# Transposing x and B for the state-space scan: on TensorE against the identity, or on DVE in blocks of 32 with a pass through DRAM

## The chip, the cores and the metric

The kernel runs on one core of a Trainium2 chip. The metric is the device time of one launch in microseconds (us). A core has five engines that work side by side, each through its own list of instructions in a fixed order: TensorE (PE in the profile, with its weight loads listed as PEld), VectorE (DVE), ScalarE (ACT), GpSimd (POOL) and SyncE (SP), which here only issues DMAs. An instruction waits for semaphores that other engines or DMAs raise; while it waits, everything behind it on the same engine waits too. DMAs move data between DRAM and the on-chip SBUF over 16 shared DMA engines ("rings" below). PSUM is the small memory that PE writes its products to.

## What is computed

One layer of a hybrid decoder, on 512 tokens (S) of 1024 channels (D), in float32: a Mamba-2 mixer and a sliding-window attention side by side, then a SwiGLU. The change touches the Mamba-2 part, the chunked scan. Cut to that:

```python
def ssd_chunked_scan(xh, dt, a, b_ssm, c_ssm):
    X = (xh * dt[..., None])                      # [chunk, T=128 tokens, group, head, 64]
    dA = dt * a
    a_cum = jnp.cumsum(dA, axis=-1)
    Lmat = jnp.exp(segsum(dA))
    CB = jnp.einsum('bclgn,bcsgn->bcgls', Cc, Bc)
    y_diag = jnp.einsum('bcgels,bcsgep->bclgep', Lmat * CB[:, :, :, None], X)
    decay_states = jnp.exp(a_cum[..., -1:] - a_cum)
    states = jnp.einsum('bclgn,bcgel,bclgep->bcgepn', Bc, decay_states, X)
    # h: running sum of states over the chunks, decayed by exp(a_cum[..., -1])
    y_off = jnp.einsum('bclgn,bcgepn,bcgel->bclgep', Cc, h_in, jnp.exp(a_cum))
    return y_diag + y_off
```

There are 4 groups of 8 heads and 4 chunks of 128 tokens, so 16 pairs of group and chunk. Each such pair is called a chunk here and numbered i = 0 to 15 (group i // 4, chunk c = i % 4 of the group).

## The kernel before

**The large products.** Every large matrix product is split into float32r halves, and one 128x512 step is three matmuls: high by high, high by low, low by high (`mm3`, L147 to L151). Weights come in units of 128x1024. The class `Units` (L110 to L145) loads a unit by SP into `w_raw` (four buffers), casts it on ACT to `w_hi` (L135) and takes the rest on DVE, `w_lo` (L136); three units are split ahead of the one in use, and four more can lie raw. One `product` (L275) is one unit: 8 steps of 3 matmuls, 24 in all, into one of three PSUM buffers of the pool psA, and then an eviction. PE's other results go to five PSUM buffers of the pool psX.

**Who sets the order.** The order on PE is the order of the code, since PE is under a manual schedule (L78). The order on DVE, ACT, POOL and SP is chosen by the scheduler from dependencies and buffers. Large products that nothing in the scan needs soon are put into a queue, the `Filler` (L153 to L183), as generators. A call `fill(us)` steps the one in front, at 0.65 us a step (one step is three matmuls); `all_done(name)` steps until all of that name are through. So the small matmuls of the scan stand on PE between blocks of filler matmuls, which cover their latency.

**The convolutions.** x, B and C of a group come from six units (`g_xbc`, L355 to L377). Their PSUM result is evicted through a causal convolution of four taps: ACT makes the first (L368, `cacc`), DVE adds three (L371), and ACT applies SiLU. This leaves channels on the partitions and tokens along the row: `bc_f` for B and C, four tiles `xs_f` for x. The six units of the next group are filler in the rounds of the present one.

**The scan.** Its main loop (L941 to L973) runs one round per chunk i. Its parts:

- `ssd_pre(i)` (L737): SP loads `L`, 512 KB, one row of DRAM broadcast to all partitions (L743), and from c = 1 on `E` in two DMAs (L750). POOL masks `L` (L754), and ACT takes 8 exps of it (L759).
- `ssd_a(i)` (L761): PE makes `ps_cb` from B and C (L774), ACT copies it to `cb`, and DVE multiplies `L` by it (L778). PE transposes the four 128x128 blocks of x by matmuls with the identity, `ps_x` (L781). DVE multiplies by dt, which gives X in two instructions (L784). For c < 3, whose state goes on, PE also transposes B (`ps_bt`, L790), ACT copies that to `bt` (L792), and POOL multiplies X by the decay, `Xd` (L795).
- `ssd_b(i)`, first half (L800): for c < 3 the state, `ps_st` = `bt` times `Xd` (L809), to which the state before is added in `h_st`; for c > 0 the part from the earlier chunks, `ps_yo` (L825). Second half: `ps_yd`, from X and L (L834), added to the output `y_g` by DVE.

Ahead of the loop stand `ssd_pre` of chunks 0 and 1, `ssd_a(0)` and a `fill(4.0)`, at which the filler's queue is still empty, so it issues nothing. A round i then calls `ssd_pre(i+2)`, `ssd_a(i+1)`, `fill`, the first half of `ssd_b(i)`, `fill`, the second half, and `fill`: 6 us each (5 in the last group). At c = 3, `all_done` makes sure that the next group's convolutions are through before `ssd_a` of its first chunk. What goes on just before the scan is the product `yb` of the attention's output, evicted into `tB` on DVE (L414).

Of the kernel before, what the change touches and what calls it, by code (L numbers as in the profile page):

```python
# [11 lines left out]
F32 = mybir.dt.float32  # L12
# [50 lines left out]
def kernel(  # L63
# [13 lines left out]
    nc = tc.nc  # L77
# [32 lines left out]
    class Units:  # L110
# [29 lines left out]
        def next(self, unit, kt=KD, ahead=None):  # L140

            assert self.order[self.pos] == unit, (self.pos, self.order[self.pos], unit)
            self.prepare(self.pos + (self.ahead if ahead is None else ahead))
            self.pos += 1
            return tuple(a.rearrange("p (k n) -> p k n", k=kt) for a in self.split.pop(self.pos - 1))  # L145
# [7 lines left out]
    class Filler:  # L153
# [19 lines left out]
        def fill(self, us):  # L173
            self.owed += us / 0.65
            while self.owed >= 1.0 and self.step():
                self.owed -= 1.0
            self.owed = min(self.owed, 1.0)
# [56 lines left out]
    h_d = dram.tile([S, D], F32, name="h_d")  # L234
    a_d = dram.tile([P, P], F32, name="a_d")
    e_d = dram.tile([P, P], F32, name="e_d")


    def xbc(g):
# [29 lines left out]
    def axt(shape, name):  # L269
        return psX.tile(shape, F32, name=name, tag="ax")  # L270
# [82 lines left out]
    xbc_t = {}  # L353
# [378 lines left out]
    er = e_d.rearrange("(g j c t) l -> g c j (t l)", g=NG, j=2, c=NT)  # L732
    dt5, dec5, cd5, nac5 = cols(dtv), cols(dec), cols(cdec), cols(nac)

    z_t, y_t, yn_t, L_t, E_t, a_t, h_t = {}, {}, {}, {}, {}, {}, {}

    def ssd_pre(i):  # L737

# [18 lines left out]
        for j in range(2):  # L757
            for t in range(4):
                nc.scalar.activation(L[:, j, t], L[:, j, t], AF.Exp, bias=nac5[:, g, j, c, t:t + 1], scale=1.0)  # L759

    def ssd_a(i):  # L761

        g, c = divmod(i, NT)
        cs = slice(c * P, (c + 1) * P)
        b_f, c_f = xbc_t[g, 0], xbc_t[g, 1]
        xs = [xbc_t[g, 2 + t] for t in range(4)]
        if c == 0:
            y = sd.tile([P, 4, S], F32, name="y_g", tag="y_g", bufs=1)
            y_t[g] = y
            for t in range(4):  # L770
                nc.scalar.mul(out=y[:, t], in_=xs[t], mul=pc[:, C_DS + 4 * g + t:C_DS + 4 * g + t + 1])
        L = L_t[i]
        ps = axt([P, P], "ps_cb")
        nc.tensor.matmul(ps, b_f[:, cs], c_f[:, cs], start=True, stop=True)  # L774
        cb = sd.tile([P, P], F32, name="cb", tag="cb", bufs=2)
        nc.scalar.copy(out=cb, in_=ps)  # L776
        Lf = L.rearrange("p j t l -> p (j t) l")
        nc.vector.tensor_tensor(out=Lf, in0=Lf, in1=cb.unsqueeze(1).broadcast_to([P, 8, P]), op=ALU.mult)  # L778
        ps = axt([P, 4, 2, 64], "ps_x")
        for t in range(4):  # L780
            nc.tensor.transpose(ps[:, t].rearrange("p j d -> p (j d)"), xs[t][:, cs], ident)  # L781
        X = sd.tile([P, 4, 2, 64], F32, name="X", tag="X", bufs=2)
        for j in range(2):
            nc.vector.tensor_tensor(  # L784
                out=X[:, :, j], in0=ps[:, :, j],
                in1=dt5[:, g, j, c].unsqueeze(2).broadcast_to([P, 4, 64]), op=ALU.mult)
        bt = Xd = None
        if c < NT - 1:
            ps = axt([P, P], "ps_bt")
            nc.tensor.transpose(ps, b_f[:, cs], ident)  # L790
            bt = sd.tile([P, P], F32, name="bt", tag="bt", bufs=2)
            nc.scalar.copy(out=bt, in_=ps)  # L792
            Xd = sd.tile([P, 4, 2, 64], F32, name="Xd", tag="Xd", bufs=2)
            for j in range(2):
                nc.gpsimd.tensor_tensor(  # L795
                    out=Xd[:, :, j], in0=X[:, :, j],
                    in1=dec5[:, g, j, c].unsqueeze(2).broadcast_to([P, 4, 64]), op=ALU.mult)
        a_t[i] = (X, bt, Xd)

    def ssd_b(i):  # L800

        g, c = divmod(i, NT)
        cs = slice(c * P, (c + 1) * P)
        y, c_f, L = y_t[g], xbc_t[g, 1], L_t.pop(i)
        X, bt, Xd = a_t.pop(i)
        h_prev = h_t.pop(g, None)
        if c < NT - 1:
            pss = axt([P, 4, 2, 64], "ps_st")
            nc.tensor.matmul(  # L809
                pss.rearrange("p t j d -> p (t j d)"), bt, Xd.rearrange("p t j d -> p (t j d)"),  # L810
                start=True, stop=True)
            h = sd.tile([P, 4, 2, 64], F32, name="h_st", tag="h_st", bufs=2)
            h_t[g] = h
            if c == 0:
                nc.scalar.copy(out=h, in_=pss)
            else:
                for j in range(2):
                    nc.gpsimd.tensor_tensor(
                        out=h[:, :, j], in0=h_prev[:, :, j],
                        in1=cd5[:, g, j, c].unsqueeze(2).broadcast_to([P, 4, 64]), op=ALU.mult)  # L820
                nc.vector.tensor_add(h, h, pss)
        if c > 0:
            pso = axt([P, 4, P], "ps_yo")
            for t in range(4):
                nc.tensor.matmul(  # L825
                    pso[:, t], h_prev[:, t].rearrange("p j d -> p (j d)"), c_f[:, cs], start=True, stop=True)
            yo = sd.tile([P, 4, P], F32, name="yo", tag="tmp", bufs=3)
            nc.vector.tensor_mul(yo, pso, E_t.pop(i))
            nc.gpsimd.tensor_add(y[:, :, cs], y[:, :, cs], yo)
        yield  # L830
        psd = axt([P, 4, P], "ps_yd")
        for t in range(4):
            for j in range(2):
                nc.tensor.matmul(  # L834
                    psd[64 * j:64 * j + 64, t], X[:, t, j], L[:, j, t], start=True, stop=True)
        nc.vector.tensor_add(y[:, :, cs], y[:, :, cs], psd)
        yield
# [97 lines left out]
    def all_done(prefix):  # L935
        while any(str(n).startswith(prefix) for n, _ in filler.q):
            filler.step()

    ssd_pre(0)
    ssd_pre(1)  # L940
    ssd_a(0)  # L941
    fill(4.0)
    norm = iter(())
    for i in range(NG * NT):
        g, c = divmod(i, NT)
        if c == 0 and g > 0:
            norm = gate_norm(g - 1)
            next(norm)
        if c == 0:
            add_stage(g)  # L950
        f0, f1, f2 = F_SSD[g]
        if i + 2 < NG * NT:
            ssd_pre(i + 2)
        if i + 1 < NG * NT:
            if c == NT - 1:
                all_done(f"x{g + 1}")
            ssd_a(i + 1)
        fill(f0)
        b = ssd_b(i)
        next(b)  # L960

        slots = (0, 1, 1) if g == NG - 1 else (2, 3, 4)
        fill(f1)
        for _ in range(slots.count(2 * c)):
            next(norm, None)
        next(b)
        fill(f2)
        for _ in range(slots.count(2 * c + 1)):
            next(norm, None)
        if c == NT - 1:  # L970
# [196 lines left out]
    for f in range(2, NF):  # L1167
        pss = []
# [101 lines left out]
```

## Time and profile before

| | us |
|---|---|
| median of 3 runs | 1028.93 |
| lowest and highest | 1028.39, 1028.96 |
| the profiled execution, in the same terms | 1028.11 |
| its span in the trace | 1026.2 |

The mean clock granted to PE in the profiled execution is 0.999 of full speed. The first transpose `ps_x` of the scan starts at 237.0 us of the span, the last at 527.2.

How to read the rows that follow. A timeline row has the start (us from the span's start), the duration, the engine or queue, the line of the kernel, the instruction with its output and inputs, the shape, and how many instructions it groups; in square brackets is the idle time ahead of it and who ended it. SPq is SP's DMA queue: its rows are issues, not transfers. A stretch row has the stretch, its length, each engine's busy time with its instructions, the granted clock, the DMA engines' busy share and GB/s. A row of groups has the engine's busy time and the mean length of one instruction. Matmuls overlap on PE, so the distance of their starts, not their duration, is what one of them takes of PE's time. A wait row names who waited, for whom, how long in all, how many times, and the longest.

### The profile page before, as it was taken

To read this page: it belongs to the slowest core of one execution; us is meant where nothing else is said; L and a number is where in the kernel's file an instruction comes from. 1 tells how busy PE (TensorE), PEld (TensorE's weight loads), DVE (VectorE), ACT (ScalarE), POOL (GpSimd) and SP (SyncE) were. 2 spreads that over 40 slices of the span, in tenths; PEclk is the share of its full clock that TensorE was granted. 3 is DMA by queue.
4 is the path that set the end of the run, shared out by engine and by line. 5 is a ranking of instruction groups with operands and counts; after the bars stand their busy time and mean duration, and the time that the engine had idled before them with its cause. 6 is when DMAs were issued, how large, how long until landed. Compare 5 with 4: busy or idle time off the path is not lost.

```text
span 1026.2 us, 13200 instructions
## 1 busy us (share of the span) xinstructions
PE 1014.5 (99%) x5044; PEld 837.6 (82%) x5044; DVE 600.5 (59%) x835; ACT 505.8 (49%) x864; POOL 205.5 (20%) x195
## 2 busy tenths in 40 slices
PE   9999999999999999999999999999999999999997
PEld 7888888887887878888888888898888888888886
DVE  6789874534656764676664595646433333332765
ACT  6464566717666885783733542434332333322450
POOL 2011223723115113111223820390000000000000
PEclk9999999999999999999999999999999999999999
DMA  8211223544443334334322344316433333331471
GB/s 317 83 64 61 88 83 104 203 142 130 136 135 106 113 116 126 106 115 138 89 93 82 123 150 179 102 42 225 144 123 123 106 120 106 120 123 62 154 255 43
DMA packets 38799, 126.56 MB, mean 123 GB/s; under 512 B 4528, under 2 KB 5040, under 8 KB 38480
## 3 DMA queue, kind: packets, MB, share of 16 engines
q1 hardware_dynamic: 36080, 116.14, 34.7%
q0 software_dynamic: 2080, 7.47, 2.0%
q10 hardware_dynamic: 576, 2.10, 0.6%
q8 instruction: 40, 0.66, 0.2%
q14 instruction: 23, 0.19, 0.1%
HBM read 119.27 MB, written 6.42 MB: 122 GB/s over the span
## 4 chain that ended last, share of the span: by engine, by line
PE 86%; DVE 4%; ACT 3%; DMA 3%; issue 2%; POOL 1%; SPq 0%; DVEq 0%; POOLq 0%; ACTq 0%
PE ps_mm L149 13%; PE ps_mm L150 12%; PE ps_mm L151 12%; PE ps_ff L151 8%; PE ps_ff L149 8%; PE ps_ff L150 8%; PE ps_da L151 2%; PE ps_da L149 2%; PE ps_da L150 2%; DMA L<-a_d 2%; PE ps_db L151 2%; PE ps_db L150 2%; PE ps_db L149 2%; PE ps_mix L149 1%; PE ps_mix L151 1%
## 5 line engine op out<-in xcount | busy, mean ns | idle before, releaser
L135 ACT CAST w_hi<-w_raw 128x1024 fp32r<-128x1024 f32 x185 | 193.4, 1051 | 305.5 <-PE ps_ff L150 123.2
L136 DVE TENSOR_TENSOR w_lo<-w_raw,w_hi 128x1024 fp32r<-128x1024 f32 x185 | 240.5, 1305 | 154.1 <-ACT w_hi L135 151.9
L149 PE MATMUL ps_mm<-hT_hi,w_hi 128*128 128x512 f32 x504 | 203.3, 403 | 1.0 <-DVE cacc L371 1.0
L150 PE MATMUL ps_mm<-hT_lo,w_hi 128*128 128x512 f32 x504 | 196.8, 391 | 0.0
L151 PE MATMUL ps_mm<-hT_hi,w_lo 128*128 128x512 f32 x504 | 196.6, 390 | 0.0
L149 PE MATMUL ps_ff<-h2T_hi,w_hi 128*128 128x512 f32 (+1 forms) x384 | 143.2, 373 | 0.0
L150 PE MATMUL ps_ff<-h2T_lo,w_hi 128*128 128x512 f32 (+1 forms) x384 | 142.6, 371 | 0.0
L151 PE MATMUL ps_ff<-h2T_hi,w_lo 128*128 128x512 f32 (+1 forms) x384 | 142.6, 371 | 0.0
L149 PEld LDWEIGHTS ps_mm<-hT_hi,w_hi 128*128 128x128 f32 x504 | 94.7, 188 | 23.1 <-issue 5.6
L151 PEld LDWEIGHTS ps_mm<-hT_hi,w_lo 128*128 128x128 f32 x504 | 94.6, 188 | 20.3
L150 PEld LDWEIGHTS ps_mm<-hT_lo,w_hi 128*128 128x128 f32 x504 | 94.8, 188 | 18.2 <-issue 1.0
L150 PEld LDWEIGHTS ps_ff<-h2T_lo,w_hi 128*128 128x128 f32 x384 | 72.3, 188 | 12.6
L151 PEld LDWEIGHTS ps_ff<-h2T_hi,w_lo 128*128 128x128 f32 x384 | 72.3, 188 | 12.5
L149 PEld LDWEIGHTS ps_ff<-h2T_hi,w_hi 128*128 128x128 f32 x384 | 72.3, 188 | 12.4
L1117 DVE TENSOR_TENSOR sgf<-sgf,ps_ff 128x512 f32<-128x512 f32 x22 | 15.1, 685 | 68.4 <-PE ps_ff L151 68.4
L149 PE MATMUL ps_mm<-yh,w_hi 128*128 128x512 f32 x124 | 49.2, 397 | 0.0
L150 PE MATMUL ps_mm<-yl,w_hi 128*128 128x512 f32 x124 | 48.3, 390 | 0.0
L151 PE MATMUL ps_mm<-yh,w_lo 128*128 128x512 f32 x124 | 48.3, 389 | 0.0
L371 DVE SCALAR_TENSOR_TENSOR cacc<-ps_mm,pc,cacc 128x511 f32<-128x511 f32 (+2 forms) x54 | 39.9, 741 | 9.8 <-ACT cacc L368 9.2
L759 ACT ACTIVATE L<-L,nac 128x128 f32<-128x128 f32 x128 | 40.9, 391 | 6.2 <-POOL L L754 5.9
L778 DVE TENSOR_TENSOR L<-L,cb 128x1024 f32<-128x1024 f32 x16 | 21.5, 1343 | 38.4 <-ACT cb L776 21.6
L754 POOL TENSOR_SCALAR_AFFINE_SELECT L<-L 128x1024 f32<-128x1024 f32 x16 | 20.1, 1256 | 93.9 <-DMA L<-a_d 93.9
(267 smaller groups left out, 1700.2 us busy)
## 6 DMA issues: line engine op xcount, KB each, us to landing
w_raw<-in_wall_dram SPq DMA_DIRECT2D x187, 512.0 KB, 3.5
L<-a_d SPq DMA_DIRECT2D x16, 512.0 KB, 5.4
E<-e_d SPq DMA_DIRECT2D x24, 128.0 KB, 3.5
x_d<-x_sb POOLq DMA_DIRECT2D x4, 512.0 KB, 7.8
row<-x_d POOLq DMA_DIRECT2D x4, 512.0 KB, 5.1
h_d<-row POOLq DMA_DIRECT2D x4, 512.0 KB, 3.0
h_r<-h_d ACTq DMA_DIRECT2D x4, 512.0 KB, 5.4
out_dram<-y_o SPq DMA_DIRECT2D x7, 256.0 KB, 4.1
```

Of the source, the lines that this page charges most:

```text
L135: (copy or nc.scalar.copy)(out=hi, in_=w)
L136: self.last = (eng or nc.vector).tensor_sub(out=lo, in0=w, in1=hi.bitcast(F32))
L149: nc.tensor.matmul(ps, lh, rh, start=start, stop=False)
L150: nc.tensor.matmul(ps, lh, rl, start=False, stop=False)
L151: nc.tensor.matmul(ps, ll, rh, start=False, stop=stop)
L371: nc.vector.scalar_tensor_tensor(out=acc[:, d:], in0=ps[:, :S - d], scalar=pc[:, cw + 3 - d:cw + 4 - d], in1=acc[:, d:], op0=ALU.mult, op1 ...
L754: nc.gpsimd.affine_select(out=Lf, in_=Lf, pattern=[[0, 8], [1, P]], compare_op=ALU.is_ge, fill=-BIG, base=0, channel_multiplier=-1)
L759: nc.scalar.activation(L[:, j, t], L[:, j, t], AF.Exp, bias=nac5[:, g, j, c, t:t + 1], scale=1.0)
L778: nc.vector.tensor_tensor(out=Lf, in0=Lf, in1=cb.unsqueeze(1).broadcast_to([P, 8, P]), op=ALU.mult)
L1117: nc.vector.tensor_mul(sg, sg, pu)
```

## The change

PE makes neither `ps_x` nor `ps_bt` any more. A new function `ssd_x(i)` has DVE transpose x in blocks of 32x32: its `transpose` swaps rows and columns inside each block but leaves the blocks where they are. The result `T` (256 KB) is written by one DMA to a DRAM scratch `t_d`, and four DMAs read it back into `R`, 32 partitions each, so that the blocks land where the transposed matrix has them, in runs of 512 bytes. For c < 3 it does the same to B, through `Tb`, `b_d` (64 KB) and four reads into `bt` in runs of 128 bytes. All these DMAs are issued by SP. A second function `ssd_dt(i)` makes X out of `R` on DVE and `Xd` on POOL, as before apart from the source.

The calls: `ssd_x(0)` stands ahead of `ssd_a(0)`, `ssd_dt(0)` and `ssd_x(1)` behind the empty `fill(4.0)`. In round i, behind the first half of `ssd_b(i)`, stand `ssd_dt(i+1)` and `ssd_x(i+2)`. `ssd_x` of a group's first chunk needs the group's convolutions, so the `all_done` for them is called in the round of c = 2, not c = 3. `T` uses three buffers that other temporaries of the scan use too (tag "tmp"), `R` has one, `bt` two as before, and `Xd` one in place of two. Line numbers in the rows of the changed kernel are those of the changed file.

```diff
@@ -234,6 +234,8 @@
     h_d = dram.tile([S, D], F32, name="h_d")
     a_d = dram.tile([P, P], F32, name="a_d")
     e_d = dram.tile([P, P], F32, name="e_d")
+    t_d = dram.tile([NG * NT, P, 4, P], F32, name="t_d")
+    b_d = dram.tile([NG * NT, P, 4, 32], F32, name="b_d")
 
 
     def xbc(g):
@@ -732,7 +734,7 @@
     er = e_d.rearrange("(g j c t) l -> g c j (t l)", g=NG, j=2, c=NT)
     dt5, dec5, cd5, nac5 = cols(dtv), cols(dec), cols(cdec), cols(nac)
 
-    z_t, y_t, yn_t, L_t, E_t, a_t, h_t = {}, {}, {}, {}, {}, {}, {}
+    z_t, y_t, yn_t, L_t, E_t, R_t, X_t, Xd_t, bt_t, h_t = ({} for _ in range(10))
 
     def ssd_pre(i):
 
@@ -758,6 +760,52 @@
             for t in range(4):
                 nc.scalar.activation(L[:, j, t], L[:, j, t], AF.Exp, bias=nac5[:, g, j, c, t:t + 1], scale=1.0)
 
+    def ssd_x(i):
+
+        g, c = divmod(i, NT)
+        cs = slice(c * P, (c + 1) * P)
+
+        T = sd.tile([P, 4, 4, 32], F32, name="T", tag="tmp", bufs=3)
+        for t in range(4):
+            nc.vector.transpose(T[:, :, t], xbc_t[g, 2 + t][:, cs])
+
+        R = sd.tile([P, 4, 4, 32], F32, name="R", tag="R", bufs=1)
+        R_t[i] = R
+        nc.sync.dma_start(out=t_d[i], in_=T.rearrange("p b t s -> p b (t s)"))
+        for b in range(4):
+            nc.sync.dma_start(
+                out=R[32 * b:32 * b + 32].rearrange("r a t s -> r a (t s)"),
+                in_=t_d[i, :, b].rearrange("(a r) x -> r a x", r=32))
+        if c < NT - 1:
+            Tb = sd.tile([P, P], F32, name="Tb", tag="Tb", bufs=1)
+            nc.vector.transpose(Tb, xbc_t[g, 0][:, cs])
+            bt = sd.tile([P, P], F32, name="bt", tag="bt", bufs=2)
+            bt_t[i] = bt
+            nc.sync.dma_start(out=b_d[i], in_=Tb.rearrange("p (b s) -> p b s", b=4))
+            for b in range(4):
+                nc.sync.dma_start(
+                    out=bt[32 * b:32 * b + 32].rearrange("r (a s) -> r a s", a=4),
+                    in_=b_d[i, :, b].rearrange("(a r) s -> r a s", r=32))
+
+    def ssd_dt(i):
+
+        g, c = divmod(i, NT)
+        R = R_t.pop(i)
+        X = sd.tile([P, 4, 2, 64], F32, name="X", tag="X", bufs=2)
+        X_t[i] = X
+        for j in range(2):
+            nc.vector.tensor_tensor(
+                out=X[:, :, j].rearrange("p t (h s) -> p t h s", h=2),
+                in0=R[:, 2 * j:2 * j + 2].rearrange("p h t s -> p t h s"),
+                in1=dt5[:, g, j, c].unsqueeze(2).unsqueeze(3).broadcast_to([P, 4, 2, 32]), op=ALU.mult)
+        if c < NT - 1:
+            Xd = sd.tile([P, 4, 2, 64], F32, name="Xd", tag="Xd", bufs=1)
+            Xd_t[i] = Xd
+            for j in range(2):
+                nc.gpsimd.tensor_tensor(
+                    out=Xd[:, :, j], in0=X[:, :, j],
+                    in1=dec5[:, g, j, c].unsqueeze(2).broadcast_to([P, 4, 64]), op=ALU.mult)
+
     def ssd_a(i):
 
         g, c = divmod(i, NT)
@@ -776,38 +824,17 @@
         nc.scalar.copy(out=cb, in_=ps)
         Lf = L.rearrange("p j t l -> p (j t) l")
         nc.vector.tensor_tensor(out=Lf, in0=Lf, in1=cb.unsqueeze(1).broadcast_to([P, 8, P]), op=ALU.mult)
-        ps = axt([P, 4, 2, 64], "ps_x")
-        for t in range(4):
-            nc.tensor.transpose(ps[:, t].rearrange("p j d -> p (j d)"), xs[t][:, cs], ident)
-        X = sd.tile([P, 4, 2, 64], F32, name="X", tag="X", bufs=2)
-        for j in range(2):
-            nc.vector.tensor_tensor(
-                out=X[:, :, j], in0=ps[:, :, j],
-                in1=dt5[:, g, j, c].unsqueeze(2).broadcast_to([P, 4, 64]), op=ALU.mult)
-        bt = Xd = None
-        if c < NT - 1:
-            ps = axt([P, P], "ps_bt")
-            nc.tensor.transpose(ps, b_f[:, cs], ident)
-            bt = sd.tile([P, P], F32, name="bt", tag="bt", bufs=2)
-            nc.scalar.copy(out=bt, in_=ps)
-            Xd = sd.tile([P, 4, 2, 64], F32, name="Xd", tag="Xd", bufs=2)
-            for j in range(2):
-                nc.gpsimd.tensor_tensor(
-                    out=Xd[:, :, j], in0=X[:, :, j],
-                    in1=dec5[:, g, j, c].unsqueeze(2).broadcast_to([P, 4, 64]), op=ALU.mult)
-        a_t[i] = (X, bt, Xd)
 
     def ssd_b(i):
 
         g, c = divmod(i, NT)
         cs = slice(c * P, (c + 1) * P)
-        y, c_f, L = y_t[g], xbc_t[g, 1], L_t.pop(i)
-        X, bt, Xd = a_t.pop(i)
+        y, c_f = y_t[g], xbc_t[g, 1]
         h_prev = h_t.pop(g, None)
         if c < NT - 1:
             pss = axt([P, 4, 2, 64], "ps_st")
             nc.tensor.matmul(
-                pss.rearrange("p t j d -> p (t j d)"), bt, Xd.rearrange("p t j d -> p (t j d)"),
+                pss.rearrange("p t j d -> p (t j d)"), bt_t.pop(i), Xd_t.pop(i).rearrange("p t j d -> p (t j d)"),
                 start=True, stop=True)
             h = sd.tile([P, 4, 2, 64], F32, name="h_st", tag="h_st", bufs=2)
             h_t[g] = h
@@ -828,6 +855,7 @@
             nc.vector.tensor_mul(yo, pso, E_t.pop(i))
             nc.gpsimd.tensor_add(y[:, :, cs], y[:, :, cs], yo)
         yield
+        X, L = X_t.pop(i), L_t.pop(i)
         psd = axt([P, 4, P], "ps_yd")
         for t in range(4):
             for j in range(2):
@@ -938,8 +966,11 @@
 
     ssd_pre(0)
     ssd_pre(1)
+    ssd_x(0)
     ssd_a(0)
     fill(4.0)
+    ssd_dt(0)
+    ssd_x(1)
     norm = iter(())
     for i in range(NG * NT):
         g, c = divmod(i, NT)
@@ -952,12 +983,16 @@
         if i + 2 < NG * NT:
             ssd_pre(i + 2)
         if i + 1 < NG * NT:
-            if c == NT - 1:
-                all_done(f"x{g + 1}")
             ssd_a(i + 1)
         fill(f0)
         b = ssd_b(i)
         next(b)
+        if i + 1 < NG * NT:
+            ssd_dt(i + 1)
+        if i + 2 < NG * NT:
+            if c == NT - 2:
+                all_done(f"x{g + 1}")
+            ssd_x(i + 2)
 
         slots = (0, 1, 1) if g == NG - 1 else (2, 3, 4)
         fill(f1)
```

On PE, the start of the scan reads before as follows (`ident` is the identity, `hT` the layer's input, `attT` the attention's output; the last row is the first of the filler):

```order
L151 MATMUL ps_mm<-attT_hi,w_lo 128x512
L774 MATMUL ps_cb<-bc_f 128x128
L781 MATMUL ps_x<-ident,xs_f 128x128 x4
L790 MATMUL ps_bt<-ident,bc_f 128x128
L774 MATMUL ps_cb<-bc_f 128x128
L781 MATMUL ps_x<-ident,xs_f 128x128 x4
L790 MATMUL ps_bt<-ident,bc_f 128x128
L149 MATMUL ps_mm<-hT_hi,w_hi 128x512
```

After, only the two `ps_cb` are left between the same two neighbours, and the rest of PE's list is the same but for the missing `ps_x` and `ps_bt`.

On DVE, the same place before, from the last eviction of `yb` on (the numbers are those of buffers, so `X_2243` is X of chunk 0, `X_2279` X of chunk 1, `L_2199` and `L_2212` the L of chunks 0 and 1, `cacc_2321` the first convolution of the next group):

```order
L414 TENSOR_TENSOR tB_639<-tB_639,ps_mm_2159 128x512
L784 TENSOR_TENSOR X_2243<-ps_x_2238,dtv_95 128x4x64 x2
L136 TENSOR_TENSOR w_lo_2294<-w_raw_2096,w_hi_2293 128x1024
L784 TENSOR_TENSOR X_2279<-ps_x_2274,dtv_95 128x4x64 x2
L778 TENSOR_TENSOR L_2199<-L_2199,cb_2235 128x1024
L778 TENSOR_TENSOR L_2212<-L_2212,cb_2271 128x1024
L371 SCALAR_TENSOR_TENSOR cacc_2321<-ps_mm_2290,pc_79,cacc_2321 128x511
```

And after, from the last transpose of chunk 1 on, ahead of which stand the other transposes of chunks 0, 1 and 2 and one `w_lo` (`X_2259` and `R_2235` belong to chunk 0, `X_2361` and `R_2270` to chunk 1, `Tb_2378` to chunk 2):

```order
L781 STREAM_TRANSPOSE Tb_2276<-bc_f_612 128x128
L826 TENSOR_TENSOR L_2201<-L_2201,cb_2256 128x1024
L826 TENSOR_TENSOR L_2214<-L_2214,cb_2302 128x1024
L373 SCALAR_TENSOR_TENSOR cacc_2337<-ps_mm_2306,pc_79,cacc_2337 128x511
L136 TENSOR_TENSOR w_lo_2348<-w_raw_2130,w_hi_2347 128x1024
L797 TENSOR_TENSOR X_2259<-R_2235,dtv_97 128x4x64 x2
L373 SCALAR_TENSOR_TENSOR cacc_2337<-ps_mm_2306,pc_79,cacc_2337 128x510
L373 SCALAR_TENSOR_TENSOR cacc_2337<-ps_mm_2306,pc_79,cacc_2337 128x509
L781 STREAM_TRANSPOSE Tb_2378<-bc_f_612 128x128
L797 TENSOR_TENSOR X_2361<-R_2270,dtv_97 128x4x64 x2
```

X of chunk 0 has moved from the front of the scan to behind both products with `cb`, the first step of a convolution and a `w_lo`.

On SP's queue, the start of the scan before:

```order
L743 DMA L_2199<-a_d_82 128x2x512
L743 DMA L_2212<-a_d_82 128x2x512
L750 DMA E_2214<-e_d_83 64x512 x2
L743 DMA L_2253<-a_d_82 128x2x512
L750 DMA E_2255<-e_d_83 64x512 x2
L120 DMA w_raw_2329<-in_wall_dram 128x1024
```

And after (the first `t_d`, `b_d`, `R` and `bt` of each name belong to chunk 0, the second to chunk 1; `L_2284` is chunk 2's):

```order
L745 DMA L_2201<-a_d_82 128x2x512
L745 DMA L_2214<-a_d_82 128x2x512
L752 DMA E_2216<-e_d_83 64x512 x2
L774 DMA t_d_84<-T_2230 128x512
L784 DMA b_d_85<-Tb_2241 128x128
L774 DMA t_d_84<-T_2265 128x512
L745 DMA L_2284<-a_d_82 128x2x512
L776 DMA R_2235<-t_d_84 32x4x128 x4
L786 DMA bt_2243<-b_d_85 32x4x32 x4
L784 DMA b_d_85<-Tb_2276 128x128
L752 DMA E_2286<-e_d_83 64x512
L776 DMA R_2270<-t_d_84 32x4x128 x4
```

The writes and reads of the scratch stand between the loads of the scan, and the reads of chunk 0, which must wait for its write, behind the load of chunk 2's L.

## The prediction

> **What bounds the kernel now.** I read the page's shares of busy time first, then its chain of the work that ended last, then the engines' busy time in stretches of the stage that the change touches.
>
> ```profile
> span 1026.2 us, 13200 instructions
> PE 1014.5 (99%) x5044; PEld 837.6 (82%) x5044; DVE 600.5 (59%) x835; ACT 505.8 (49%) x864; POOL 205.5 (20%) x195
> PE 86%; DVE 4%; ACT 3%; DMA 3%; issue 2%; POOL 1%; SPq 0%; DVEq 0%; POOLq 0%; ACTq 0%
> 270.00:300.00 30.00, 30.00 (x160) 24.20 (x160) 21.43 (x25) 21.33 (x34) 4.85 (x5) 1.00 0.36 108
> 330.00:360.00 30.00, 30.00 (x147) 23.81 (x145) 23.01 (x29) 25.70 (x37) 5.12 (x6) 1.00 0.36 119
> ```
>
> The columns of the last two rows are the stretch, its length, then busy time of PE, PEld, DVE, ACT and POOL, the granted clock, the DMA share and GB/s. PE (TensorE) is busy in all 30 us of both stretches and has 86% of the chain. So two things count: PE time removed is saved one for one, and any wait put on PE is paid one for one. DVE still has 7 us of 30 free in the fuller stretch.
>
> **What is removed.** A matmul's duration is not its cost, since matmuls overlap. The cost is read from starts that follow each other in the timeline of PE; the rows show the block of chunk 2 (start, duration, instruction).
>
> ```profile
> 259.76 0.39 PE L151 MATMUL ps_mm<-hT_hi,w_lo 128*128 128x512 f32 x1
> 259.99 0.38 PE L774 MATMUL ps_cb<-bc_f 128*128 128x128 f32 x2
> 260.21 0.60 PE L781 MATMUL ps_x<-ident,xs_f 128*128 128x128 f32 x4
> 260.64 0.27 PE L790 MATMUL ps_bt<-ident,bc_f 128*128 128x128 f32 x1
> 260.67 0.47 PE L149 MATMUL ps_mm<-hT_hi,w_hi 128*128 128x512 f32 x1
> 260.99 0.39 PE L150 MATMUL ps_mm<-hT_lo,w_hi 128*128 128x512 f32 x1
> ...
> L781 PE MATMUL ps_x<-ident,xs_f x64: 272/273/273, 237.0 to 527.2; 128*128 128x128 f32 x64
> ...
> L790 PE MATMUL ps_bt<-ident,bc_f x12: 272/273/300, 237.4 to 507.9; 128*128 128x128 f32 x12
> ...
> PE ps_yo L825 <- DVE X L784: 0.5, 1, 0.5
> PE ps_bt L790 <- DVE X L784: 0.2, 1, 0.2
> ```
>
> Four `ps_x` transposes take 260.21 to 260.64, 0.43 us. A 512-wide matmul follows the last one 0.23 us later (259.76 to 259.99); the step from `ps_bt` to the second `ps_mm` is 0.35, so `ps_bt` costs 0.12. Sixteen chunks have `ps_x` (64 matmuls), twelve have `ps_bt`: 16 x 0.43 + 12 x 0.12 = 8.3 us. The two waits for X on the old PSUM path go too: 0.7 us. Together **9.0 us saved**. The order of PE is otherwise the same, matmul for matmul: the earlier call for the next group's convolutions forces nothing, since some 42 us of filler at 0.65 us a step, 64 steps, precede it and the six units have 48. So what is late next can only be a wait.
>
> [...]
>
> **What is added at the start of the stage.** Chunk 0 is the only one whose round trip has no earlier chunk to hide behind. `ps_st` of chunk 0 stands on PE behind `ps_cb` twice and 30 filler matmuls, and needs `Xd` and `bt`; everything on PE stands behind it. Here is the same start in the timelines of before.
>
> ```profile
> 236.78 0.38 PE L774 MATMUL ps_cb<-bc_f 128*128 128x128 f32 x2
> ...
> 238.66 0.48 PE L149 MATMUL ps_mm<-hT_hi,w_hi 128*128 128x512 f32 x1
> ...
> 245.60 1.02 PE L809 MATMUL ps_st<-Xd,bt 128*128 128x512 f32 x2
> ...
> 236.97 0.90 SPq L743 DMA_DIRECT2D L<-a_d  x2
> 237.92 2.08 SPq L750 DMA_DIRECT2D E<-e_d  x2
> 240.04 0.98 SPq L743 DMA_DIRECT2D L<-a_d  x1
> ...
> 242.03 1.09 POOL L754 TENSOR_SCALAR_AFFINE_SELECT L<-L 128x1024 f32<-128x1024 f32 x1 [1.07 <-DMA L<-a_d]
> ...
> 244.66 1.09 POOL L754 TENSOR_SCALAR_AFFINE_SELECT L<-L 128x1024 f32<-128x1024 f32 x1 [0.96 <-DMA L<-a_d]
> 248.15 1.09 POOL L754 TENSOR_SCALAR_AFFINE_SELECT L<-L 128x1024 f32<-128x1024 f32 x1 [2.40 <-DMA L<-a_d]
> ...
> 243.24 4.99 ACT L759 ACTIVATE L<-L,nac 128x128 f32<-128x128 f32 x16
> ...
> 251.63 0.76 ACT L368 ACTIVATE cacc<-ps_mm,pc 128x512 f32<-128x512 f32 x1
> 252.30 1.03 ACT L135 CAST w_hi<-w_raw 128x1024 fp32r<-128x1024 f32 x1
> ...
> 237.70 0.76 DVE L784 TENSOR_TENSOR X<-ps_x,dtv 128x256 f32<-128x256 f32 x2
> ...
> 248.32 2.00 DVE L778 TENSOR_TENSOR L<-L,cb 128x1024 f32<-128x1024 f32 x1 [1.31 <-ACT L L759]
> ...
> 256.33 1.22 DVE L136 TENSOR_TENSOR w_lo<-w_raw,w_hi 128x1024 fp32r<-128x1024 f32 x1
> 257.46 0.74 DVE L371 SCALAR_TENSOR_TENSOR cacc<-ps_mm,pc,cacc 128x510 f32<-128x510 f32 x1
> ...
> L795 POOL TENSOR_TENSOR Xd<-X,dec x24: 603/613/1586, 238.2 to 514.6; 128x256 f32<-128x256 f32 x24
> ```
>
> PE comes to it early: the two `ps_cb` take 4 x 0.11 from 236.78, and the 30 matmuls took 245.60 - 238.66 = 6.94, so it is **due at 244.2**. Two chains lead to X.
>
> The first is on the engines. In the new DVE order X of chunk 0 stands behind both products L x cb, the first `cacc` and a `w_lo`. ACT ends the exps of chunks 0 and 1 at 243.24 + 4.99 = 248.2, as before; then `cacc` 0.76 to 249.0 and the cast 1.03 to 250.0. DVE: the second product from 248.3 (1.23 to 2.00) to 249.6 or 250.3, `cacc` 0.74, `w_lo` 1.22, so X begins at 251.5 to 252.3, although 237.70 was enough before.
>
> The second goes through DRAM. SP issues `t_d` of chunk 0 at 240.0, behind L, L and E. No row shows a DVE transpose; the nearest is X, twice the columns in 0.38 us each. I take 0.28 and keep 0 and 0.76 as bounds: the four of chunk 0, from 237.7 on, end at 238.8, or at 240.7 at worst, so they delay `t_d` by 0.7 at most, behind rings that are busy until later anyway. The transfers go through the rings in the order of their issue: from the landing of the second L, 244.66, to the third, 248.15, 256 KB of E and 512 KB of L took 3.5 us, so 4.6 us per 1000 KB. E and `t_d` (256 KB each) land at 244.66 + 2.3 = 247.0; only then may R's four reads be issued. Ahead of them are then `b_d`, the second `t_d` and the third L, 832 KB, to 250.8. R has 256 KB in 512-byte runs: 1.2 us by bytes, up to 5 us if a run costs what a 2 KB run of L costs (512 runs against 256 in 2.4). `bt`, 64 KB in 128-byte runs behind it: 0.3 to 5 us. R lands at 252.0 to 255.8, `bt` at 252.3 to 260.8.
>
> X (0.76) and two `Xd` (1.2) follow R or the DVE chain, whichever is later: `ps_st` can begin at 254.3 at the earliest and at 260.8 at the latest. I take R's landing at 253.4, a third of the way up, since L's runs are one DRAM row read 128 times over, a dearer kind than R's, which all differ. `ps_st` then begins at 255.4: **11.2 us of wait on PE**, bounds 10.1 and 16.6. If the rings serve nothing ahead of R, the DVE chain alone still gives 253.5, a wait of 9.3.
>
> After such a gap PE may be slow. At the kernel's start PE has idled as well:
>
> ```profile
> 0.00:4.00 4.00, 2.47 (x12) 2.47 (x13) 0.39 (x1) 3.07 (x4) 3.28 (x18) 1.00 0.50 153
> 4.00:6.00 2.00, 2.00 (x11) 2.00 (x10) 1.53 (x5) 0.29 (x1) 0.73 (x2) 1.00 0.97 309
> 6.00:8.00 2.00, 2.00 (x18) 2.00 (x17) 0.00 (x0) 1.98 (x2) 0.42 (x1) 1.00 0.98 360
> ```
>
> 23 equal matmuls took 4.47 us, then 18 took 2.00: at the later pace the 23 take 2.56, so **1.9 us** is lost, bounds 0 and 1.9. The granted clock reads 1.00 in all three rows, so only the pace shows it. [...]
>
> **What is added later, and its cover.** In each further round, `ssd_x` of chunk i+2 runs inside round i.
>
> ```profile
> w_raw<-in_wall_dram SPq DMA_DIRECT2D x187, 512.0 KB, 3.5
> ...
> 282.86 0.38 PE L774 MATMUL ps_cb<-bc_f 128*128 128x128 f32 x2
> ```
>
> A round trip is 9 us: 3.5 for the write and again for the read, the landing of a `w_raw` of twice the size, then X and `Xd`, 2.0. With the dearest runs it is 14. `ps_cb` came at 259.99 and at 282.86, so a round lasts 22.9 us and covers it. R has one buffer, and its reads wait for the X before; that X is a round old. Behind SP's wait for `t_d` stand weight loads; 3 split and 4 raw units lie ahead of PE, and a unit is 24 x 0.227 = 5.4 us, so 7 us of delay is hidden. Behind DVE's wait for R stand evictions of three PSUM buffers, two units or 10.9 us deep. DVE gets 76 transposes, some 21 us over 320, out of the 7 in 30 that it has free. ACT loses twelve copies. If this cover fails, each of the 15 later chunks costs PE what is missing.
>
> **Sum.** 1028.1 (profiled execution, of which 1026.2 is span) - 9.0 + 11.2 + 1.9 = 1032.2. The median of the runs shown, 1028.9, is 0.8 above the profiled one; the same sum on it is 1033.0. I forecast 1032.5.
>
> **Rivals.** *The start is covered*: chunk 0's X arrives early. It decides from where `ps_st` can begin before 244.2 + 9.0 - 1.9 = 251.3; fully covered the time is 1028.9 - 9.0 = 1019.9, faster. For it: `t_d` can be issued at 240.0. Against it: `cacc` and `w_lo` ahead of X on DVE, which no DMA speeds up. *Durations are the cost*: 76 transposes free 76 x 0.273 = 20.7 us and the start costs 13.1, giving 1020.6; the starts 0.11 us apart speak against it. [...] *Small runs are dear, everywhere*: each run costs what L's does, the start costs 16.6 + 1.9, and the later round trips of 14 us meet evictions that wait behind X on DVE; with no later loss 1028.9 - 9.0 + 18.5 = 1038.4, with 0.5 us in each of 15 chunks 1046.
>
> **How the numbers follow.** About 0.2%, 2.1 us, is what a measurement here can tell from no change. The forecast case, a wait of 9.3 to 14 at the start, has 0.68 and spans 1029 to 1036; its low end, without the slow pace, lies within 0.2% (0.12). Dear runs 0.20; start covered 0.09; durations 0.03. Faster 0.12, same 0.12, slower 0.76. The range 1028 to 1042 holds the forecast case and most of the dear runs.
>
> **What would show it.** In the changed kernel's waits of PE one entry should stand out: `ps_st` for POOL's `Xd` or the DMA of `bt`, once, 9 to 17 us, near 244; the matmuls behind it at a slower pace for some 4 us; elsewhere PE full. DVE's X of chunk 0 should start after 251. The forecast is wrong if PE does not stop there, or stops in most rounds.

## The result

| | before | changed |
|---|---|---|
| median of 6 runs, us | 1028.71 | 1032.01 |
| lowest and highest | 1028.11, 1028.96 | 1030.65, 1033.33 |
| profiled execution | 1028.11 | 1031.27 |
| its span | 1026.2 | 1029.5 |

The ratio of changed to before is 1.0036, with a 95% interval of 1.0026 to 1.0047: slower by 2.7 to 4.8 us, 3.3 in the medians, where 1032.5 was forecast for the changed kernel. Of the executions further down, one of the filled wait (3631 us) and one with more filler (1693 us) were slow ones and are left out of the times and ratios given.

The page of the changed kernel has its span, the busy time of each engine, and the granted clock in 40 slices of 25.7 us:

```profile
span 1029.5 us, 13358 instructions
PE 1008.2 (98%) x4968; PEld 830.0 (81%) x4968; DVE 616.8 (60%) x911; ACT 499.2 (48%) x848; POOL 207.4 (20%) x195
PEclk9999999998999999999999999999999999999999
```

From its waits of PE, the two longest of those that lie in the scan's rounds (who waited, for whom, how long in all, how often, the longest):

```profile
PE ps_st L836 <- POOL Xd L805: 10.0, 1, 10.0
...
PE ps_mm L149 <- DVE cacc L373: 0.7, 1, 0.7
```

PE has 76 matmuls fewer and 6.3 us less busy time, yet the span is longer. There is one wait of 10.0 us, once, and no other in the scan reaches 1 us. The clock's one digit below 9 is in the slice of that wait. PE's timeline at the place:

```profile
244.28 0.39 PE L151 MATMUL ps_mm<-hT_hi,w_lo 128*128 128x512 f32 x1
254.64 2.08 PE L836 MATMUL ps_st<-Xd,bt 128*128 128x512 f32 x2 [9.97 <-POOL Xd L805]
255.72 1.42 PE L149 MATMUL ps_mm<-hT_hi,w_hi 128*128 128x512 f32 x1
256.94 0.63 PE L150 MATMUL ps_mm<-hT_lo,w_hi 128*128 128x512 f32 x1
257.37 0.63 PE L151 MATMUL ps_mm<-hT_hi,w_lo 128*128 128x512 f32 x1
257.79 0.63 PE L149 MATMUL ps_mm<-hT_hi,w_hi 128*128 128x512 f32 x1
258.22 0.46 PE L150 MATMUL ps_mm<-hT_lo,w_hi 128*128 128x512 f32 x1
...
258.75 0.40 PE L149 MATMUL ps_mm<-hT_hi,w_hi 128*128 128x512 f32 x1
...
261.95 0.39 PE L151 MATMUL ps_mm<-hT_hi,w_lo 128*128 128x512 f32 x1
```

The matmul at 244.28 takes 0.23, so `ps_st` was due at 244.5 and began at 254.64: 10.1 us. Behind it starts are 0.43 apart at first and 0.23 later. The stretches of the same kernel (stretch, length, busy time of PE, PEld, DVE, ACT, POOL, granted clock, DMA share, GB/s) show the clock that goes with it, at half for some 4 us:

```profile
244.00:255.00 11.00, 1.03 (x4) 0.57 (x4) 6.76 (x10) 9.17 (x27) 4.40 (x5) 0.69 0.58 178
255.00:257.00 2.00, 2.00 (x4) 0.87 (x4) 0.24 (x2) 1.93 (x3) 0.00 (x0) 0.50 0.42 110
257.00:259.00 2.00, 2.00 (x8) 1.57 (x7) 0.72 (x2) 0.46 (x1) 1.46 (x3) 0.66 0.29 60
```

In the same trace the clock reads 1.00 from 245 to 247, 0.50 from 249 to 253, all of it time in which PE stands still, and 1.00 again from 259 to 261. PE's starts are 0.23 apart from 258.52 on, 3.9 us behind `ps_st`.

How long did PE lose there? From before, a timeline row (the 21st `ps_mm` behind `ps_st`, as the one at 261.95 is after) and the row of the tile `ps_ms`, whose last start is at the scan's end:

```profile
251.03 0.39 PE L151 MATMUL ps_mm<-hT_hi,w_lo 128*128 128x512 f32 x1
...
L863 PE MATMUL ps_ms<-sqr,ones_r x8: 392/403/404, 344.7 to 572.2; 128*128 128x512 f32 x8
```

And the latter row after:

```profile
L891 PE MATMUL ps_ms<-sqr,ones_r x8: 392/403/405, 352.6 to 575.7; 128*128 128x512 f32 x8
```

From `ps_st` to the 21st `ps_mm` before took 251.03 - 245.60 = 5.43, after 261.95 - 254.64 = 7.31: **1.88 us** lost by the slow pace. From there to the last `ps_ms` before took 572.2 - 251.03 = 321.2, after 575.7 - 261.95 = 313.8: **7.4 us** gained in the 14 later chunks. From the first `ps_cb` (236.78 before, 237.25 after) to `ps_st` it is 8.82 and 17.39, 8.57 more, which is the wait of 10.1 less 1.5 for the transposes of chunks 0 and 1. So 10.1 + 1.9 - 1.5 - 7.4 = 3.1, the 3.2 by which the profiled executions differ.

What held `Xd` is in the timelines of SP, DVE and POOL:

```profile
240.50 0.83 SPq L774 DMA_DIRECT2D t_d<-T  x1
...
247.47 1.75 SPq L776 DMA_DIRECT2D R<-t_d  x4
249.32 1.80 SPq L786 DMA_DIRECT2D bt<-b_d  x4
...
247.93 1.18 DVE L826 TENSOR_TENSOR L<-L,cb 128x1024 f32<-128x1024 f32 x1
249.62 1.23 DVE L826 TENSOR_TENSOR L<-L,cb 128x1024 f32<-128x1024 f32 x1 [0.50 <-issue]
250.76 0.75 DVE L373 SCALAR_TENSOR_TENSOR cacc<-ps_mm,pc,cacc 128x511 f32<-128x511 f32 x1
251.42 1.45 DVE L136 TENSOR_TENSOR w_lo<-w_raw,w_hi 128x1024 fp32r<-128x1024 f32 x1
252.79 0.75 DVE L797 TENSOR_TENSOR X<-R,dtv 128x256 f32<-128x256 f32 x2
...
253.29 1.29 POOL L805 TENSOR_TENSOR Xd<-X,dec 128x256 f32<-128x256 f32 x2 [1.50 <-DVE X L797]
```

The tile R has the time from issue to landing of its eight reads of chunks 0 and 1:

```profile
DMA to landing us min/median/max: 1.8/2.1/2.6
```

R's reads were issued from 247.47 on, when `t_d` had landed; the fourth at about 248.8. None took over 2.6, so R was there by 251.4. X stood until 252.79, with no idle time of DVE right ahead of it: DVE was at the two products, `cacc` and `w_lo`. DVE's order set X, with R 1.4 us ahead of it. That chain hung on ACT in turn: the second product began at 249.62, when ACT had ended the exps of chunk 1 (247.09 + 2.44 = 249.53).

### The profile page after: what moved, and what is told of

Same layout as the page of the kernel before. It is cut to its first block, busy times and chain, and to the rows that moved or that the text cites. A ratio compares the mean times of both kernels' runs of the same rounds, so it can differ in the third digit from the quotient of the medians.

```text
span 1029.5 us, 13358 instructions
## 1 busy us (share of the span) xinstructions
PE 1008.2 (98%) x4968; PEld 830.0 (81%) x4968; DVE 616.8 (60%) x911; ACT 499.2 (48%) x848; POOL 207.4 (20%) x195
## 4 chain that ended last, share of the span: by engine, by line
PE 88%; DVE 4%; ACT 3%; DMA 3%; issue 1%; POOL 1%; SPq 0%; ACTq 0%; POOLq 0%; DVEq 0%
PE ps_mm L149 13%; PE ps_mm L150 13%; PE ps_mm L151 13%; PE ps_ff L151 8%; PE ps_ff L149 8%; PE ps_ff L150 8%; PE ps_da L151 2%; PE ps_da L149 2%; PE ps_da L150 2%; PE ps_db L150 2%; PE ps_db L151 2%; PE ps_db L149 2%; PE ps_mix L149 1%; PE ps_mix L151 1%; PE ps_mix L150 1%; DMA L<-a_d 1%
## 5 line engine op out<-in xcount | busy, mean ns | idle before, releaser
L149 PEld LDWEIGHTS ps_ff<-h2T_hi,w_hi 128*128 128x128 f32 x384 | 72.3, 188 | 12.4
L150 PE MATMUL ps_da<-w_lo,hA_hi 128*128 128x512 f32 x88 | 34.2, 389 | 0.0
```

The source lines that it names most:

```text
L149: nc.tensor.matmul(ps, lh, rh, start=start, stop=False)
L150: nc.tensor.matmul(ps, lh, rl, start=False, stop=False)
```

## The experiments

They ran in three sets, each beside the kernel before: 1027.7 us there (chunk 0 on PE, chunk 0 early, filled wait, X first), 1028.2 (the changed kernel again, `Xd` on DVE, trip first, more filler) and 1028.1 (the other three). So sets are compared by their ratios to it.

**Is the start all that the change costs?** Chunk 0 alone gets its transposes on PE again, at the end of `ssd_a`:

```diff
-    ssd_x(0)
     ssd_a(0)      # for i == 0: ps_x, X, ps_bt, bt, Xd as before
     fill(4.0)
-    ssd_dt(0)
     ssd_x(1)
```

> Chunk 0 alone gets its x and B transposed by PE against the identity, as before; chunks 1 to 15 stay as changed. Theory A (all that the change costs is one wait of 10.0 us at ps_st of chunk 0 and 1.9 us of slow pace behind it, and the transposes are worth 0.55 us a chunk everywhere): 1032.0 - 10.0 - 1.9 + 0.55 = 1020.7, and no wait of PE over 1 us in the scan. Theory B (the wait only moves on: chunk 1's trip through DRAM is now 11 us nearer to its use): a wait at ps_st of chunk 1 of 2 us or more, 1023 to 1028.

Measured: 1020.82, ratio 0.993 (0.9918 to 0.9943); theory A's 1020.7 is a ratio of 0.9922. PE's waits in the scan are one of 0.9 us and smaller ones; none is at `ps_st`. The wait did not move on to chunk 1.

**Is the whole saving there without it?** Chunk 0's transposes and trip are made during the `yb` products, from a copy of `ssd_x`; R and `bt` come from a pool that is open by then:

```diff
     for f in range(KD):
         filler.add("yb", g_yb(f))
+    need("gb")
+    for _ in range(16):
+        filler.step()
+    ssd_x0()
...
-    ssd_x(0)
     ssd_a(0)
```

> Chunk 0's transposes on DVE and its trip through DRAM are made some 30 us ahead, during the yb products; no transpose is on PE anywhere. Theory A: R and bt of chunk 0 lie ready, X of chunk 0 is made at about 238, PE does not stop at ps_st, and the whole saving is left: 1028.7 - 9.0 = 1019.7. Theory B (later chunks have too little cover once PE comes 11 us earlier): waits of PE in later rounds, 1022 or more.

Measured: 1019.2, ratio 0.9916 (0.9903 to 0.993), and run once more beside other kernels

> The kernel with chunk 0's transposes and trip through DRAM made early, once more, beside the next two. Every theory: 9.0 us below the time before of this chip, to within 0.7.

1019.85, ratio 0.9917 (0.9904 to 0.9931). That is 8.5 and 8.2 us below before (the second 0.1 outside what was expected), with 9.0 inside both intervals, and the fastest kernel here. The two longest of PE's waits in the first of the two:

```profile
PE ps_warm L547 <- POOL ident masks.py:199: 1.5, 1, 1.5
PE ps_mm L149 <- ACT yacc L961: 0.6, 1, 0.6
```

The longest left stands at the kernel's very start. In the second the wait for `yacc` is 1.2 and one for `cacc` 0.7; neither is at `ps_st`. Theory B falls: the later rounds have their cover even when PE comes earlier.

**What is a transpose worth?** To that kernel the four transposes of x are added again in every chunk, ahead of `ps_st`, with nobody to read them, so that no other engine gets work by it:

```diff
     def ssd_b(i):
...
+        ps = axt([P, 4, P], "ps_x2")
+        for t in range(4):
+            nc.tensor.transpose(ps[:, t], xbc_t[g, 2 + t][:, cs], ident)
```

> The same, with the four transposes of x of every chunk put on PE again ahead of each ps_st, where nobody reads their result: 64 matmuls added to a PE that waits for nothing. Theory A (their price is the distance of starts, 0.43 us for four): 16 x 0.43 = 6.9 us more. Theory F (their price is their duration, 0.273 each): 64 x 0.273 = 17.5 us more.

Measured: 1026.7, ratio 0.9988 (0.9979 to 0.9997), beside 1019.85: 6.85 us for 64 matmuls, 0.107 each. PE's waits in the scan differ by under 1 us between the two (1.2 in all here, 1.9 there), so their price is the distance of their starts. The rival by durations, 17.5, is out.

**Is the slow pace due to the idle time?** The wait is filled with matmuls whose result nobody reads:

```diff
         fill(f0)
+        if i == 0:
+            ps = axt([P, S], "ps_warm2")
+            for _ in range(44):
+                nc.tensor.matmul(ps, hT_hi[:, 0, 0:P], hT_hi[:, 0], start=True, stop=True)
         b = ssd_b(i)
```

> 44 matmuls 128x512 whose result nobody reads stand ahead of ps_st of chunk 0, 44 x 0.227 = 10.0 us, so PE is busy for the whole of what was its wait; all else as changed. Theory A (PE is slow behind the gap because it stood idle): the wait falls from 10.0 to about 0.2, the granted clock stays 1.00 in this stretch, and the time falls by the 1.9 us alone: 1030.1. Theory D (the slow pace has another cause, such as the transfers that run then): no change, 1032.0.

Measured: 1029.98, ratio 1.0024 (1.0014 to 1.0033). The interval holds A's 1.0014 at its edge and D's 1.0032, so the total does not decide; the stretches do (columns as before):

```profile
244.00:255.00 11.00, 11.00 (x50) 9.13 (x49) 6.02 (x9) 10.12 (x27) 4.84 (x5) 1.00 0.65 190
255.00:257.00 2.00, 2.00 (x9) 1.30 (x8) 0.95 (x2) 1.22 (x2) 0.33 (x1) 1.00 0.42 121
257.00:259.00 2.00, 2.00 (x11) 1.61 (x10) 0.76 (x2) 1.20 (x3) 0.72 (x2) 1.00 0.25 43
```

The clock stays at 1.00, with transfers at about the same rate, and 9 matmuls are in the stretch from 255 to 257 where there were 4. From `ps_st` to the 21st `ps_mm` it is 5.43 us, as before the change: no slow pace is left. It comes from the gap.

**Which chain held X?** On DVE the second product, the evictions and the weight splits of round 0 are issued behind X of chunk 0:

```diff
+        with held():          # issue_after(X of chunk 0) in round 0
             nc.vector.tensor_tensor(out=Lf, in0=Lf, in1=cb..., op=ALU.mult)
# the same around w_lo (L136) and the three taps of cacc (L373)
```

> On DVE the second product L x cb, the first convolution steps and the weight splits of round 0 are put behind X of chunk 0; DMAs as changed. Theory A (DVE's order sets X of chunk 0, since R's last read was issued at 249.2 and landed some 2 us later, about 251.3, while X began at 252.8): X begins at 251.3, ps_st at 253.2, the wait is 8.6 us, 1.4 less, 1030.6. Theory C (R's landing sets it, as the prediction took it): X stays at 252.8, the wait at 10.0, 1032.0.

Measured: 1031.44, ratio 1.0035 (1.0021 to 1.0048): no gain. Its timelines of PE, DVE and POOL:

```profile
243.94 0.39 PE L157 MATMUL ps_mm<-hT_hi,w_lo 128*128 128x512 f32 x1
253.56 2.07 PE L844 MATMUL ps_st<-Xd,bt 128*128 128x512 f32 x2 [9.23 <-POOL Xd L812]
...
250.72 0.76 DVE L804 TENSOR_TENSOR X<-R,dtv 128x256 f32<-128x256 f32 x2 [2.42 <-DMA R<-t_d]
251.40 1.63 DVE L834 TENSOR_TENSOR L<-L,cb 128x1024 f32<-128x1024 f32 x1
...
251.23 2.27 POOL L812 TENSOR_TENSOR Xd<-X,dec 128x256 f32<-128x256 f32 x2 [0.47 <-DVE X L804]
```

This execution runs 0.34 ahead (243.94 for 244.28). X now waits for R and came 1.7 us earlier, more than A said: DVE's order had held it. But the two `Xd` took 2.27 us beside the product on DVE, which took 1.63, so `ps_st` began only 0.7 earlier. A wait for `cacc` of 1.2 us in place of 0.7, and 2.2 us by the slow pace in place of 1.9, took that back.

To see whether POOL ate the gain, `Xd` of chunk 0 is made by DVE right behind X:

```diff
-                nc.gpsimd.tensor_tensor(
+                ins = (nc.gpsimd if i else nc.vector).tensor_tensor(
                     out=Xd[:, :, j], in0=X[:, :, j], ...)
```

> As with X of chunk 0 put first on DVE, and Xd of chunk 0 is made by DVE right behind X, not by POOL. Theory A (where X was put first, POOL's two Xd took 2.27 us beside DVE's product L x cb, against 1.2 to 1.3 elsewhere, and that ate most of the gain): the two take 0.8 on DVE, ps_st begins when bt lands, some 1.2 us earlier than there, a wait of 8.0 us. Rival: bt lands later than Xd, and the wait stays at 9.2.

Measured: 1029.77, ratio 1.0013 (1.0004 to 1.0022); the wait, still for `Xd`, fell to 7.8 us. On its timeline of DVE X again follows R's landing, the two `Xd` take 0.75, and the product takes its usual 1.22:

```profile
251.02 0.76 DVE L804 TENSOR_TENSOR X<-R,dtv 128x256 f32<-128x256 f32 x2 [2.12 <-DMA R<-t_d]
251.70 0.75 DVE L812 TENSOR_TENSOR Xd<-X,dec 128x256 f32<-128x256 f32 x2
252.37 1.22 DVE L836 TENSOR_TENSOR L<-L,cb 128x1024 f32<-128x1024 f32 x1
```

**How much of the trip is what stands ahead of it in the rings?** With X first, and with L and E of chunk 1 behind chunk 0's writes and reads:

```diff
     ssd_pre(0)
-    ssd_pre(1)
     ssd_x(0)
+    with tc.issue_after(x_dma[0].ins):      # the last read of bt
+        ssd_pre(1)
     ssd_a(0)
```

> As with X of chunk 0 put first on DVE, and also the writes and reads of chunk 0 are issued ahead of L and E of chunk 1, so that only L of chunk 0 is ahead of t_d in the rings. Theory A (the write of t_d took 6.9 us to land because L, L and E were ahead of it, by some 4.6 us per 1000 KB): t_d lands near 243.5, R near 247.5, X follows the first product L x cb near 249.1 at the latest, ps_st begins by 251.1, the wait is 4.5 to 6.7 us, and the time falls by 3 to 5 us against the changed kernel. Theory E (the trip is slow by itself, by its own short runs): t_d takes 6 us or more to land again, the wait stays at 8.5 or more, the time falls by less than 1.5.

Measured: 1027.9, ratio 0.9996 (0.9987 to 1.0005), a wait of 5.9 us, still for `Xd`. SP, DVE and POOL on its timeline:

```profile
238.80 0.34 SPq L783 DMA_DIRECT2D t_d<-T  x1
...
243.22 1.75 SPq L785 DMA_DIRECT2D R<-t_d  x4
...
247.54 0.75 DVE L806 TENSOR_TENSOR X<-R,dtv 128x256 f32<-128x256 f32 x2
248.21 1.63 DVE L142 TENSOR_TENSOR w_lo<-w_raw,w_hi 128x1024 fp32r<-128x1024 f32 x1
...
248.04 2.27 POOL L814 TENSOR_TENSOR Xd<-X,dec 128x256 f32<-128x256 f32 x2 [4.30 <-DVE X L806]
```

R's reads followed `t_d` after 4.4 us (238.80 to 243.22) where it was 7.0 (240.50 to 247.47). Theory A's mechanism and size hold, with a wait within 4.5 to 6.7 and a time 4.1 us below that of the changed kernel; theory E falls. The changed kernel itself, beside these:

> The changed kernel itself, beside the next three on one chip. Every theory: the ratio of 1.0036 again, and the wait of 10 us at ps_st of chunk 0.

Measured: 1031.99, ratio 1.0032 (1.002 to 1.0043), a wait of 9.4 us at `ps_st`, 9.6 by the starts (10.0 and 10.1 in the first execution). DVE's order set X here too, at 252.00. The slow pace was longer: `ps_st` to the 21st `ps_mm` took 8.28 us, 2.85 more than before, with starts 0.43 apart until 259.56.

**Useful work in the gap.** Round 0 issues 75 filler matmuls ahead of `ps_st`, not 30:

```diff
-        f0, f1, f2 = F_SSD[g]
+        f0, f1, f2 = F_SSD[g] if i else (16.0, 1.0, 1.0)
```

> In round 0 the filler ahead of ps_st is 16 us in place of 6 (75 matmuls in place of 30), and the two later ones 1 us each in place of 6, so that useful work fills the wait; all else as changed. Theory A: ps_st is due at 237.6 + 17.0 = 254.6, when Xd is there, so wait and slow pace are both gone: the time before less 9.0, to within 0.5 us. Theory B (DVE's queue is the real limit: evictions of the convolutions stand behind X of chunk 0, and three PSUM buffers are not enough for 75 matmuls): waits of 1 us or more at ps_mm in round 0, 2 to 5 us above that.

Measured: 1022.61, ratio 0.9946 (0.9932 to 0.9959). The start is clean, with no wait at `ps_st`. But against the kernel with chunk 0 early (0.9917) 3 us of the gain are missing, and of these 2.1 stand at one place:

```profile
PE ps_mm L149 <- ACT z L870: 2.1, 1, 2.1
```

This is the eviction of a `z` product, 100 us later. With 0.9 for `yacc` and 0.6 for `cacc`, of which 0.3 in round 0, PE's waits in the scan are 3.6 us, where the first profile with chunk 0 early has 0.8; that is nearly all of the 3. B's mechanism, convolutions behind X in round 0, is the 0.3 at most. The timelines show what made ACT late: an exp of an `L` stands ahead of that eviction and waited 3.7 us for the load of `L`, which SP issued at 346.06, behind a write of `t_d`; with chunk 0 early SP issued it ahead of that write, at 343.99. The kernel with transposes added has the same order and waits 1.2 us at the same place. No run changed that order alone, so this cause is read and not tried.

**How thin is the later cover?** In the kernel with chunk 0 early, each later trip is called a round later:

```diff
-    ssd_x(1)
...
         if i + 1 < NG * NT:
+            if c == NT - 1:
+                all_done(f"x{g + 1}")
+            ssd_x(i + 1)
             ssd_dt(i + 1)
-        if i + 2 < NG * NT:
-            if c == NT - 2:
-                all_done(f"x{g + 1}")
-            ssd_x(i + 2)
```

> The kernel with chunk 0 early, but every later chunk's transposes and trip are called one round later, right ahead of its ssd_dt, so that a trip has some 18 us of filler until its ps_st in place of 41. Theory A (a trip is 9 us, with X and Xd 11, and 18 cover it): no wait of PE over 1.5 us, within 1 us of the kernel with chunk 0 early. Theory G (the cover is thin, since evictions and weight splits queue behind X on DVE): waits of PE in several rounds, 3 us or more above it.

Measured: 1032.29, ratio 1.0041 (1.0028 to 1.0054), 12.4 us above the kernel with chunk 0 early. Neither theory: not several rounds, but one, chunk 4.

```profile
PE ps_st L863 <- POOL Xd L832: 10.6, 1, 10.6
PE ps_mm L149 <- DVE cacc L373: 1.5, 1, 1.5
```

SP and DVE on its timeline:

```profile
308.52 0.33 SPq L801 DMA_DIRECT2D t_d<-T  x1
312.56 1.75 SPq L803 DMA_DIRECT2D R<-t_d  x4
...
319.71 0.69 DVE L231 TENSOR_TENSOR sqr<-sq,sqr 128x512 fp32r<-128x512 f32 x1 [3.14 <-ACT sqr L230]
320.32 0.89 DVE L797 STREAM_TRANSPOSE T<-xs_f 128x128 f32<-128x128 f32 x4
321.12 0.72 DVE L824 TENSOR_TENSOR X<-R,dtv 128x256 f32<-128x256 f32 x2
```

The expectation had counted filler that is not there. Group 0 has 10 units, 80 steps, and its rounds take 28 steps each, so the fourth round finds the filler empty, and chunk 4's trip starts in it. R's four reads were out at 314.3, yet X came at 321.12, behind the gating's `sqr` and another chunk's transposes on DVE. The wait of 10.6 and a slow pace of 2.85 (`ps_st` to the 21st `ps_mm`: 8.28 us) are 13.5 of the 13.9 us by which the two profiled executions differ (1033.77 and 1019.85). In the other rounds no wait passes 1.5 us, so there the shorter cover was enough.

## Why the prediction was right

**The saving** (9.0 forecast) was 1.5 + 7.4 = 8.9 by the starts. The price by starts is shown by the added transposes: 6.85 us for 64.

**One stop, at `ps_st` of chunk 0, for `Xd`.** As forecast in place and cause: due at 244.2 (244.5 after), once, and no other step of the scan waited 1 us. That it is all the loss is shown from both sides: chunk 0 back on PE, and chunk 0 early.

**Its size** was forecast as 11.2 and measured, by the starts, as 10.1 and 9.6. The step that was off is the choice of R's landing, 253.4, as the later of the two chains. R was there by 251.4, earlier than the lower bound given for it, 252.0. The third L, which is ahead of R in the rings, landed at 249.9, when POOL's mask of it began, and not at 250.8. In the two runs where X waits for R, it began 1.1 and 1.3 us after that mask; R's bytes had been put at 1.2 us, so its runs of 512 bytes cost no more than their bytes. That L's runs are a dearer kind, since they repeat one DRAM row, was an argument: before, the rings moved 239 GB/s at a share of 1.01 with L and E under way (246 to 248) and 360 at 0.98 with neither (6 to 8), but no run tests the cause. So DVE's chain decided; it had been put at 251.5 to 252.3, and X began at 252.79, of which 0.5 is the later start of the scan (`ps_cb` at 237.25 for 236.78), and at 252.00 in the second execution. The bounds, 9.3 by DVE alone and 10.1 to 16.6 by the rings, held both measured waits, so the sum survived the wrong binder.

**What stands ahead of `t_d`** was right: in the changed kernel the first two L landed at 242.8 and 245.9, `t_d` at 247.4, the third L by 249.9 and R from 250.1 on, in the order of their issue. The landing of `t_d` was forecast at 247.0, R's reads were issued at 247.47, and putting it first took 2.6 us off.

**The slow pace** was forecast as 1.9, with that as its upper bound, and measured as 1.88, but this agreement is luck: the same kernel's second execution lost 2.85, X first 2.2, and the trip a round later 2.85. The row it came from was misread, too. A stretch row counts a matmul that crosses its edge in both stretches, and starts twice as far apart as later went on past 6.00. This is the row of that line of the kernel before, from 0 to 6.6 us:

```profile
L545 PE MATMUL ps_warm<-ident x24: 331/421/477, 1.5 to 6.5; 128*128 128x128 f32 x24
```

These 24, up to the start of the 25th at 6.66, took 5.1 us where the later pace gives 2.6: a loss of 2.5. There the clock column had read 1.00; behind the wait it reads 0.50.

**DVE's transposes** were taken at 0.28 each without a row:

```profile
L770 DVE STREAM_TRANSPOSE T<-xs_f 128x128 f32<-128x128 f32 x64 | 14.3, 277 | 0.0
```

**The later cover** held, as forecast. It is less even than the forecast's one number, 22.9 us for a round, says: the call two rounds ahead is what carries chunk 4 over the round without filler.

Together -8.9 + 10.1 + 1.9 = 3.1, where the forecast had -9.0 + 11.2 + 1.9 = 4.1; with the second execution's wait and slow pace it is -8.9 + 9.6 + 2.9 = 3.6. The mechanism was the one forecast. That the total came within 0.5 us is luck in part, since a wait put too long and a slow pace put too short offset each other. Of the rivals, the covered start fell by the wait itself, the price by durations by the added transposes, and the dear small runs by R's landing.

## What to carry to other kernels

Work moved from the bounding engine to a longer path saves its price on every step that has cover (here 8.9 us over the 16 chunks), and costs the whole latency on the first step, which has none (here a wait of 10.1 us): start that one early, or leave it where it was. Here this turned 3.3 us of loss into 8 of gain. A matmul's price, on a PE that is never idle, is the distance of starts (here 0.107 us for a transpose that lasts 0.273), and a cover must be counted in the filler that is still queued at that point, not in rounds.

## What was not expected of the hardware

DVE and POOL stood in each other's way. `Xd`, two instructions of POOL, took 1.29 us beside `cacc` on DVE, but 2.27 beside the product L x cb and again beside `w_lo`; and those took 1.63 in place of 1.23. The two `Xd` with X first on DVE (shortest, median and longest in ns, then the first and last start):

```profile
L812 POOL TENSOR_TENSOR Xd<-X,dec x2: 723/1154/1584, 251.2 to 251.9; 128x256 f32<-128x256 f32 x2
```

One `Xd` alone takes 0.61. The first, from 251.23, took 0.72. L x cb, begun at 251.40, took 0.41 more than its 1.22 and ended at 253.03. The second `Xd`, begun at 251.9, took 1.58 and ended at 253.50, 0.47 behind L x cb. Why the two slow each other, and `cacc` and `Xd` hardly do, no run tests. With `Xd` on DVE the two took 0.75 and the product 1.22. The changed kernel pays a little of this on the path to X: POOL's mask of the third L took 1.89 in place of 1.09 beside the second product, and `w_lo` behind it 1.45 in place of 1.2.
